# The last products of a two-layer backbone, taken a quarter of the tokens at a time for all four column tiles

## The chip, the cores and the metric

The program runs on one core of a Trainium2 chip. The metric is device time in microseconds (us) of one execution, over several executions of the same program; the trace is of one execution taken with the hardware profiler. The engines are named as the profile names them: PE is TensorE (matrix products), DVE is VectorE, ACT is ScalarE, POOL is GpSimd, SP is SyncE, whose queue issues the transfers.

## What is computed

Two layers over 1024 tokens of 1024 features, then a final RMS norm. Only the end of it matters here: the output projection of the second layer, the gated residual and the norm.

```python
def rmsnorm(x, g):
    xf = x.astype(jnp.float32)
    y = xf * lax.rsqrt(jnp.mean(xf * xf, axis=-1, keepdims=True) + RMS_EPS)
    return (y * g.astype(jnp.float32)).astype(x.dtype)
...
    return (y * jax.nn.silu(g)) @ p["w_out"]
...
        x = x + gate[:, None] * out_x
...
    return rmsnorm(x, final_g)
```

The norm of a token needs its squares over all 1024 features, so no output of a token can be written before its last feature is done.

## The kernel before

Features lie on the partitions, in eight column tiles of 128 (x[0] to x[7], 128 x 1024 tokens each); tokens lie along the free axis. HALF[0] is tokens 0 to 511, HALF[1] tokens 512 to 1023; `first` is 512 to 767 and `second` 768 to 1023, each a quarter of all tokens.

**Products.** A matrix product is made of 2 x 2 blocks by a scheme with seven block products. One pair of column tiles (m and m+1) and both halves of the tokens come out of the seven. Each block product (`prod`, L897 to L904) is 12 matmuls: four pieces of the inner dimension, and for each high x high, high x low and low x high parts of the operands. `last_half0` (L1546) makes five of the seven for one pair and so finishes HALF[0] of that pair. What is left for HALF[1] of a pair are two products: t1 (weights w[4]), whose result, copied out of the accumulator, completes tile m+1, and b22 (weights w[2]), accumulated on top of it, which completes tile m. The last two pairs are tiles 4, 5 (weights wa) and 6, 7 (weights wb).

**After a product.** `p5` (L1591) issues t1, has ACT copy the accumulator into a tile s3 (L1594), has DVE add gate times s3 to x (`gated`, L1422) and ACT square it (L1498). `p3` (L1598) issues b22 onto the same accumulator, which must therefore wait until the copy s3 has been read out, and then the same gated add, from PSUM, and a square. `fin_add` (L1504) adds a square to the sum `fin` of its half, on DVE.

**Norm.** `fin_cols` (L1507) sums `fin` over the partitions with small PE matmuls against ones (L1512, 128 tokens each) and takes the square root on ACT (`rc`, L1515). `fin_root` (L1518) takes the reciprocal and spreads it into a diagonal (`dg`), both on DVE (through `ordered`, L1494), broadcasts it over the partitions with a PE matmul (L1525) and copies that broadcast to SBUF on ACT (`rr`, L1527). `fin_out` (L1531) multiplies: tiles 1, 2, 3 on POOL with the copy rr (L1539), tiles 0, 4, 5, 6, 7 on DVE with the broadcast in PSUM (L1494), and stores groups of tiles with eight transfers on SP's queue (L1544), 512 KB each. DVE's first scaling of a root comes after ACT's copy of that root in the program's waits.

**What sets the order.** Each engine works its instructions in one fixed order. A scheduler lays that order out before the run; two chains in the code tie its hands. `product` (L1586) chains the block products in the order in which they are written, and `ordered` (L1490) chains DVE's adds, sums, reciprocals and scalings likewise. Before the change the written order is: t1 of tiles 4, 5 for the whole half (512 columns), t1 of tiles 6, 7 for each quarter, b22 of tiles 4, 5 for the whole half, b22 of tiles 6, 7 for each quarter. The root of HALF[0] and its scalings are written between these; the roots of the two quarters come after all of them.

Of the kernel before, what the change touches and what calls it, by code (L numbers as in the profile page):

```python
# [21 lines left out]
H = 512  # L22
HALF = (slice(0, H), slice(H, S))
# [32 lines left out]
def body(ctx, tc, xT, ctxT, cc, ccol, modT, modW, win, gw, wout, wu, grp, wg, wo1, small, edge, ident, outT):  # L56
# [18 lines left out]
    def dtile(name, dt=F32):  # L75
        return dpool.tile([P, S], dt, tag="d", name=name)
# [4 lines left out]
    def ttile(name):  # L81
        return tpool.tile([P, H], F32, tag="t", name=name)
# [4 lines left out]
    def psum(name):  # L87
        return pm.tile([P, H], F32, tag="mm", name=name)
# [27 lines left out]
    def wload(src, name, eng, n=D, out=None):  # L116
        raw = wpool.tile([P, n], F32, tag="wr", name=f"wr_{name}")
        load(raw, src)
        if out is None:
            hi = wpool.tile([P, n], F32R, tag="wh", name=f"wh_{name}")  # L120
            lo = wpool.tile([P, n], F32R, tag="wl", name=f"wl_{name}")
        else:
            hi, lo = out(f"wh_{name}", F32R), out(f"wl_{name}", F32R)
        split(raw, hi, lo, eng)
        return hi, lo
# [22 lines left out]
    def col(o, n=1):  # L148
        return sm[:, o : o + n]
# [326 lines left out]
    def raw_split(raw, name):  # L476
        hi = wpool.tile([P, D], F32R, tag="wh", name=f"wh_{name}")
        lo = wpool.tile([P, D], F32R, tag="wl", name=f"wl_{name}")
        cast(hi, raw)
        gp(out=lo, in0=raw, in1=hi.bitcast(F32), op=sub)  # L480
        return hi, lo
# [113 lines left out]
    with ExitStack() as actx:  # L595
# [77 lines left out]
        w = wload(win[3 * KT], "xb0", nc.gpsimd)  # L673
# [5 lines left out]
        w = wload(win[KT], "vg0", nc.gpsimd)  # L679
# [4 lines left out]
        for j in range(KT):  # L684
# [27 lines left out]
            if state is None:  # L712
                for m in range(2 * KT, 3 * KT):
                    part = L[m % 6][:, :D]
# [45 lines left out]
            for n, _ in enumerate(gate_steps(j, (gwh, gwl), (uh, ul), gates)):  # L760
# [3 lines left out]
                if n == 9:  # L764
                    w = raw_split(raw, name)
# [146 lines left out]
    def quad(w, name, ops, put, ahead=None):  # L912
        p1, p2, p3, p4, p5, p6, p7 = w
        a, c, b = psum(f"qa_{name}"), psum(f"qc_{name}"), psum(f"qb_{name}")
        prod(a, p1, ops["b11"], True, False)
        with tc.high_priority(offset=EVAC):
            evac = nc.scalar.copy(b, a)
        prod(c, p5, ops["t1"], True, False)
        with tc.high_priority(offset=EVAC):
            put(1, 1, c, 0)  # L920
        prod(b, p6, ops["t2"], False, False)
        with tc.high_priority(offset=EVAC):
            put(0, 1, b, 0)
        prod(a, p2, ops["b21"], False, True)
        with tc.high_priority(offset=EVAC):
            put(0, 0, a, None)
        w = None
        if ahead is not None:
            with tc.issue_after(evac.ins):
                w = ahead()  # L930
        prod(b, p7, ops["t3"], False, False)
        with tc.high_priority(offset=EVAC):
            put(1, 1, b, 1)
        prod(c, p3, ops["b22"], False, True)
        with tc.high_priority(offset=EVAC):
            put(0, 1, c, 1)
        prod(b, p4, ops["t4"], False, True)
        with tc.high_priority(offset=EVAC):
            put(1, 0, b, None)
        return w  # L940
# [90 lines left out]
    for m in range(KT):  # L1031
        w = gws[KT + m]
# [84 lines left out]
    for i in range(KH):  # L1117
        for j in (i, KH + i) if i else ():
            w = wload(win[2 * KT + j], f"ga{j}", nc.gpsimd)
# [224 lines left out]
    def wo1_weights(part, m):  # L1344
        return wquad([wo1[m + i, part] for i in range(2)], f"wo{part}_{m}", wo1_ring,
                     part == 1 and m >= KT - 4)
# [3 lines left out]
    for m in range(0, NK, 2):  # L1350
# [38 lines left out]
        elif m <= KT:  # L1389
            n = 2 * KT + m - 2  # L1390
# [9 lines left out]
        w = quad(wq, f"g{m}", bx, to_gate, (lambda: wo1_weights(0, 0)) if m == NK - 2 else None)  # L1400
# [24 lines left out]
    for m in range(0, KT, 2):  # L1425
# [28 lines left out]
        w = quad(w, f"wo0_{m}", yops[0], put, nxt)  # L1454
# [10 lines left out]
    for m in range(0, KT - 4, 2):  # L1465
# [12 lines left out]
        w = quad(w, f"wo1_{m}", yops[1], put, ahead)  # L1478
# [11 lines left out]
    def ordered(f, *args, **kw):  # L1490
        with ExitStack() as octx:
            if after[0] is not None:
                octx.enter_context(tc.issue_after(after[0].ins))
            after[0] = f(*args, **kw)  # L1494

    def square(k, cols):
        q = ttile(f"fq{k}_{cols.start}")[:, : cols.stop - cols.start]
        nc.scalar.activation(q, x1[k][:, cols], AF.Square)  # L1498
        return q
# [7 lines left out]
    def fin_cols(cols, ps):  # L1507
        n, h = cols.stop - cols.start, cols.start // H
        off, nt = cols.start - h * H, n // P
        sums = ps[0][:, :nt]  # L1510
        for c in range(nt):
            nc.tensor.matmul(sums[:, c : c + 1], fin[h][:, off + c * P : off + (c + 1) * P], ones[:, 0:1],  # L1512
                             start=True, stop=True)
        r = hpool.tile([P, nt], F32, tag=f"rc_{cols.start}", name=f"rc_{cols.start}")
        nc.scalar.activation(r, sums, AF.Sqrt, bias=eps_r)  # L1515
        return ps[1][:, -n:], r

    def fin_root(cols, root, r):  # L1518
        n = root.shape[-1]
        ordered(nc.vector.reciprocal, r, r)  # L1520
        t = ttile(f"dg_{cols.start}")[:, :n]
        ordered(nc.vector.tensor_tensor, out=t.rearrange("p (c t) -> p c t", t=P),
                in0=idD.unsqueeze(1).to_broadcast([P, n // P, P]),
                in1=r.unsqueeze(2).to_broadcast([P, n // P, P]), op=mult)
        nc.tensor.matmul(root, ones, t, start=True, stop=True)  # L1525
        rr = dtile(f"rr_{cols.start}")[:, :n]
        nc.scalar.copy(rr, root)  # L1527
        return root, rr


    def fin_out(cols, root, rr):  # L1531
        n = cols.stop - cols.start
        per = D // n
        for k0 in range(0, KT, per):
            o = dtile(f"o{cols.start}_{k0}").rearrange("p (k n) -> p k n", n=n)
            for k in range(k0, k0 + per):
                v = x1[k][:, cols]
                if k in GAINED:
                    nc.gpsimd.tensor_tensor(out=o[:, k - k0], in0=v, in1=rr, op=mult)  # L1539
                else:  # L1540
                    ordered(nc.vector.scalar_tensor_tensor, out=o[:, k - k0], in0=v, scalar=col(O_FG + k), in1=root,
                            op0=mult, op1=mult)
                    yield
            nc.sync.dma_start(outT[k0 : k0 + per, :, cols].rearrange("k p n -> p k n"), o)  # L1544
# [31 lines left out]
    m = KT - 4  # L1576
    wa = w
    wb, _, _ = last_half0(m, wa, ahead)
# [4 lines left out]
    first, second = slice(H, H + H // 2), slice(H + H // 2, S)  # L1583
    whole, local = slice(0, H), [slice(0, H // 2), slice(H // 2, H)]

    def product(w, op, c, part, start):  # L1586
        nonlocal mm
        with tc.issue_after(mm.ins):
            mm = prod_cols(c, w, ops[op], start, not start, part)

    def p5(m, w, c, part, cols):  # L1591
        product(w[4], "t1", c, part, True)
        s3 = ttile(f"s3_l{m}_{cols.start}")[:, : cols.stop - cols.start]
        nc.scalar.copy(s3, c[:, part])  # L1594
        ordered(gated, m + 1, x1[m + 1][:, cols], s3)
        return square(m + 1, cols)

    def p3(m, w, c, part, cols):  # L1598
        product(w[2], "b22", c, part, False)
        ordered(gated, m, x1[m][:, cols], c[:, part])  # L1600
        return square(m, cols)

    c4, c6 = psum("qc_l"), [psum(f"qc_l{n}") for n in range(2)]
    q5 = p5(m, wa, c4, whole, HALF[1])
    sums0 = fin_cols(HALF[0], fps[0])
    q7 = [p5(m + 2, wb, c6[0], local[0], first)]
    ordered(fin_add, HALF[1], q5)
    q7.append(p5(m + 2, wb, c6[1], local[1], second))
    root0 = fin_root(HALF[0], *sums0)
    q4 = p3(m, wa, c4, whole, HALF[1])  # L1610
    ordered(fin_add, first, q7[0])
    ordered(fin_add, second, q7[1])
    ordered(fin_add, HALF[1], q4)
    out0 = fin_out(HALF[0], *root0)
    q6 = [p3(m + 2, wb, c6[0], local[0], first)]
    next(out0)
    ordered(fin_add, first, q6[0])
    sums1 = fin_cols(first, fps[1])
    next(out0)
    q6.append(p3(m + 2, wb, c6[1], local[1], second))  # L1620
    next(out0)
    ordered(fin_add, second, q6[1])
    sums2 = fin_cols(second, [psum("fin_ms2")] * 2)
    root1 = fin_root(first, *sums1)
    for _ in out0:
        pass
    root2 = fin_root(second, *sums2)
    for cols, root in ((first, root1), (second, root2)):
        for _ in fin_out(cols, *root):
            pass  # L1630


def layout(i):
# [85 lines left out]
```

## Time and profile before

| | us |
|---|---|
| median of 3 runs | 1341.01 (1340.15 to 1341.77) |
| the profiled execution | 1340.89 |
| its span, first to last instruction | 1339.1 |
| mean granted TensorE clock | 0.985 |
| part of the span after the last block product's last matmul began (1321.81) | 17.3 |

The profile's page gives the busy time of each engine; the timeline gives single instructions with their start and length in us from the span's start, and in brackets the idle time of the engine just before and what ended it. A matmul's length includes a drain of 0.16 us that the next matmul does not wait for: the start-to-start distance is its cost on PE. A stage table gives, for each stretch of time, its length, each engine's busy time and count of instructions, the granted clock (PEclk), the share of the transfer engines and GB/s.

### The profile page before, as it was taken

What the parts mean: (1) busy time and instruction counts of PE and PEld (TensorE: products, weight loads), DVE (VectorE), ACT (ScalarE), POOL (GpSimd) and SP (SyncE); (2) the same over time, 40 slices, a digit from 0 to 9 for tenths busy, and PEclk for the clock granted to TensorE, in tenths of its full rate; (3) what the DMA queues carried; (4) which work ended last, traced back from release to release, by engine and by line L of the source; (5) the groups of instructions that cost most, each with busy time, mean ns of one, the idle gap of its engine ahead of it and who ended that gap; (6) DMA issues with size and microseconds to landing.
All of it is one profiled execution on the core that took longest, in us unless ns stands there. A gap on an engine that the chain in (4) does not pass through costs nothing.

```text
span 1339.1 us, 15886 instructions
## 1 busy us (share of the span) xinstructions
PE 1275.7 (95%) x5664; PEld 1039.6 (78%) x5664; DVE 1155.6 (86%) x1775; ACT 639.7 (48%) x924; POOL 344.1 (26%) x180
## 2 busy tenths in 40 slices
PE   7799999999999999969998999999999999999896
PEld 4478888888888887857887888788888888777684
DVE  7996999998999989999778767999999977877775
ACT  6353655666656623216534345744333434634442
POOL 5274443554436546532220023000000000000002
PEclk9999999999999999989998999999999999999997
DMA  9844111121111233432454446244333335767623
GB/s 359 295 142 165 41 47 56 56 71 40 63 56 56 79 126 115 161 126 79 155 173 141 170 172 197 87 149 150 107 115 118 116 113 163 262 213 250 220 102 126
DMA packets 82867, 181.80 MB, mean 136 GB/s; under 512 B 7778, under 2 KB 27618, under 8 KB 82788
## 3 DMA queue, kind: packets, MB, share of 16 engines
q1 hardware_dynamic: 74340, 176.60, 38.3%
q10 hardware_dynamic: 8448, 4.20, 1.1%
q8 instruction: 44, 0.72, 0.2%
q14 instruction: 35, 0.29, 0.1%
HBM read 136.72 MB, written 44.04 MB: 135 GB/s over the span
## 4 chain that ended last, share of the span: by engine, by line
PE 69%; DVE 15%; DMA 7%; ACT 3%; issue 2%; POOL 2%; SPq 0%; POOLq 0%; DVEq 0%; ACTq 0%
PE gb L445 7%; PE vg L445 6%; PE va L445 6%; PE xb L445 6%; DVE conv L445 4%; PE g L445 4%; PE wob L445 2%; PE ga L445 2%; PE ga L135 2%; PE ga L134 2%; PE ga L133 2%; DMA yr_t<-y_t 2%; DVE junk L219 2%; PE qb_g L901 1%; PE qb_g L904 1%
## 5 line engine op out<-in xcount | busy, mean ns | idle before, releaser
L445 DVE SCALAR_TENSOR_TENSOR conv<-u,sm,conv 128x505 f32<-128x505 f32 (+6 forms) x224 | 153.0, 745 | 0.8
L1539 POOL TENSOR_TENSOR o<-x,rr 128x256 f32<-128x256 f32 (+1 forms) x9 | 8.1, 933 | 457.7 <-ACT rr L1527 454.8
L445 ACT ACTIVATE l<-g,sm 128x512 f32<-128x512 f32 (+1 forms) x96 | 58.7, 619 | 58.8 <-PE g L445 58.1
L103 POOL TENSOR_TENSOR wl_wu<-wr_wu,wh_wu 128x1024 fp32r<-128x1024 f32 x16 | 38.9, 2434 | 153.9 <-ACT wh_wu L102 147.9
L256 PE MATMUL fold<-gh,wh_wu 128*128 128x512 f32 x128 | 53.4, 418 | 5.3 <-ACT wh_wu L102 5.3
L257 PE MATMUL fold<-gl,wh_wu 128*128 128x512 f32 x128 | 52.8, 413 | 3.7 <-DVE gl L103 3.7
L258 PE MATMUL fold<-gh,wl_wu 128*128 128x512 f32 x128 | 51.6, 412 | 2.5 <-POOL wl_wu L103 2.5
L445 POOL TENSOR_TENSOR l<-l,l 128x1280 f32<-128x1280 f32 x16 | 47.0, 2963 | 26.1 <-DVE conv L445 17.6
L445 PE MATMUL wob<-ybl,wh_wob 128*128 128x512 f32 x128 | 50.5, 394 | 3.0 <-POOL ybl L445 3.0
L102 ACT CAST wq_wo<-wr_wo 128x512 fp32r<-128x512 f32 x48 | 28.9, 619 | 48.4 <-DMA wr_wo<-wo 18.4
L445 PE MATMUL wob<-ybh,wh_wob 128*128 128x512 f32 x128 | 51.5, 403 | 0.0
L445 PE MATMUL wob<-ybh,wl_wob 128*128 128x512 f32 x128 | 50.1, 391 | 0.0
L445 PE MATMUL gb<-h0l,wh_gb 128*128 128x512 f32 x128 | 49.8, 389 | 0.0
L445 PE MATMUL gb<-h0h,wh_gb 128*128 128x512 f32 x128 | 49.8, 389 | 0.0
L445 PE MATMUL vg<-h0l,wh_vg 128*128 128x512 f32 x128 | 49.8, 389 | 0.0
L445 PE MATMUL vg<-h0h,wh_vg 128*128 128x512 f32 x128 | 49.8, 389 | 0.0
L445 PE MATMUL vg<-h0h,wl_vg 128*128 128x512 f32 x128 | 49.8, 389 | 0.0
L445 PE MATMUL va<-h0h,wh_va 128*128 128x512 f32 x128 | 49.8, 389 | 0.0
L445 PE MATMUL va<-h0l,wh_va 128*128 128x512 f32 x128 | 49.8, 389 | 0.0
L445 PE MATMUL va<-h0h,wl_va 128*128 128x512 f32 x128 | 49.8, 389 | 0.0
L445 PE MATMUL gb<-h0h,wl_gb 128*128 128x512 f32 x128 | 49.8, 389 | 0.0
L445 DVE TENSOR_TENSOR_SCAN l<-l,l 128x256 f32<-128x256 f32 (+1 forms) x32 | 48.7, 1521 | 1.1
(584 smaller groups left out, 4348.1 us busy)
## 6 DMA issues: line engine op xcount, KB each, us to landing
mod<-modT SPq DMA_DIRECT2D x20, 512.0 KB, 6.6
wr_wu<-wu SPq DMA_DIRECT2D x16, 512.0 KB, 4.1
x_part<-xp SPq DMA_DIRECT2D x32, 256.0 KB, 2.4
mod<-modT SPq DMA_DIRECT2D x32, 256.0 KB, 3.2
wr_v<-wfold SPq DMA_DIRECT2D x16, 512.0 KB, 3.6
wr_g<-wg SPq DMA_DIRECT2D x16, 512.0 KB, 4.9
wr_wo<-wo SPq DMA_DIRECT2D x16, 512.0 KB, 4.9
yr_t<-y_t SPq DMA_DIRECT2D x16, 512.0 KB, 6.5
```

The lines of the kernel that those rows point to most:

```text
L102: return (nc.scalar.copy(hi, src), eng.tensor_tensor(out=lo, in0=src, in1=hi.bitcast(F32), op=sub))
L103: eng.tensor_tensor(out=lo, in0=src, in1=hi.bitcast(F32), op=sub))
L133: nc.tensor.matmul(ps, hi[:, kc], xh[k][:, cols], start=(k == 0), stop=False)
L134: nc.tensor.matmul(ps, hi[:, kc], xl[k][:, cols], start=False, stop=False)
L135: nc.tensor.matmul(ps, lo[:, kc], xh[k][:, cols], start=False, stop=(k == ks - 1))
L219: nc.vector.scalar_tensor_tensor(out=junk, in0=raw, scalar=1.0, in1=vec, op0=mult, op1=mult, accum_out=t[:, i, m : m + 1])
L256: nc.tensor.matmul(ps, wh[:, kc], gh[i], start=(i == 0), stop=False)
L257: nc.tensor.matmul(ps, wh[:, kc], gl[i], start=False, stop=False)
L258: nc.tensor.matmul(ps, wl[:, kc], gh[i], start=False, stop=(i == 3))
L445: last[eng] = f(*args, **kw)
L901: nc.tensor.matmul(ps, hi, xh[k], start=(first and k == 0), stop=False, skip_group_check=not first)
L904: mm = nc.tensor.matmul(ps, lo, xh[k], start=False, stop=(k == KH - 1), skip_group_check=not first)
```

## The change

All four column tiles' products are made for one quarter of the tokens at a time: for `first` t1 of tiles 4, 5, t1 of tiles 6, 7, b22 of 4, 5, b22 of 6, 7, and then the same for `second`. So all products have 256 columns (96 matmuls of 256, where there were 24 of 512 and 48 of 256). A generator `half0`, advanced between the products of the first quarter, issues the sums, the root and the scalings of HALF[0]; `quarter0`, advanced between the products of the second quarter, issues what is left of them and then the root and scalings of the first quarter.

```diff
-    c4, c6 = psum("qc_l"), [psum(f"qc_l{n}") for n in range(2)]
-    q5 = p5(m, wa, c4, whole, HALF[1])
+
+    def quarter(cols, part, between):
+        n = cols.start // (H // 2)
+        cs = [psum(f"qc_l{q}_{n}") for q in range(2)]
+        qs = []
+        for q, w in enumerate((wa, wb)):
+            qs.append(p5(m + 2 * q, w, cs[q], part, cols))
+            next(between, None)
+        for q, w in enumerate((wa, wb)):
+            ordered(fin_add, cols, qs[q])
+            qs.append(p3(m + 2 * q, w, cs[q], part, cols))
+            next(between, None)
+        for q in (2, 3):
+            ordered(fin_add, cols, qs[q])
+
+    def half0():
+        yield
+        root0 = fin_root(HALF[0], *sums0)
+        yield
+        for _ in fin_out(HALF[0], *root0):
+            yield
+
     sums0 = fin_cols(HALF[0], fps[0])
-    q7 = [p5(m + 2, wb, c6[0], local[0], first)]
-    ordered(fin_add, HALF[1], q5)
-    q7.append(p5(m + 2, wb, c6[1], local[1], second))
-    root0 = fin_root(HALF[0], *sums0)
-    q4 = p3(m, wa, c4, whole, HALF[1])
-    ordered(fin_add, first, q7[0])
-    ordered(fin_add, second, q7[1])
-    ordered(fin_add, HALF[1], q4)
-    out0 = fin_out(HALF[0], *root0)
-    q6 = [p3(m + 2, wb, c6[0], local[0], first)]
-    next(out0)
-    ordered(fin_add, first, q6[0])
+    rest = half0()
+    quarter(first, local[0], rest)
     sums1 = fin_cols(first, fps[1])
-    next(out0)
-    q6.append(p3(m + 2, wb, c6[1], local[1], second))
-    next(out0)
-    ordered(fin_add, second, q6[1])
+
+    def quarter0():
+        next(rest, None)
+        root1 = fin_root(first, *sums1)
+        yield
+        for _ in rest:
+            yield
+        for _ in fin_out(first, *root1):
+            yield
+
+    rest1 = quarter0()
+    quarter(second, local[1], rest1)
     sums2 = fin_cols(second, [psum("fin_ms2")] * 2)
-    root1 = fin_root(first, *sums1)
-    for _ in out0:
+    for _ in range(3):
+        next(rest1, None)
+    root2 = fin_root(second, *sums2)
+    for _ in rest1:
         pass
-    root2 = fin_root(second, *sums2)
-    for cols, root in ((first, root1), (second, root2)):
-        for _ in fin_out(cols, *root):
-            pass
+    for _ in fin_out(second, *root2):
+        pass
```

What this does to the engines' orders shows at three places. In the rows below, the accumulators are named qc_l<pair>_<quarter> after the change (pair 0 is tiles 4, 5; quarter 2 is `first`, 3 is `second`); fq<tile>_<first token> is a square, s3_l<4 or 6>_<first token> a copied accumulator, fin_ms0, fin_ms1, fin_ms2 the roots of HALF[0], `first` and `second`, rr their copies, and o the scaled output.

ACT around the copy of the first root (rr_0). Before the change:

```order
L1498 ACTIVATE fq7_768_10450<-x2_7_10264 128x256
L1498 ACTIVATE fq4_512_10471<-x2_4_10148 128x512
L1527 COPY rr_0_10456<-fin_ms0_1_10389 128x512
L1498 ACTIVATE fq6_512_10489<-x2_6_10262 128x256
L1515 ACTIVATE rc_512_10496<-fin_ms1_10390,eps_r_121 128x2
L1498 ACTIVATE fq6_768_10519<-x2_6_10262 128x256
```

And ACT after the change:

```order
L1498 ACTIVATE fq4_512_10453<-x2_4_10148 128x256
L1527 COPY rr_0_10437<-fin_ms0_1_10389 128x512
L1498 ACTIVATE fq6_512_10471<-x2_6_10262 128x256
L1594 COPY s3_l4_768_10501<-qc_l0_3_10487 128x256
L1498 ACTIVATE fq5_768_10504<-x2_5_10150 128x256
L1515 ACTIVATE rc_512_10485<-fin_ms1_10390,eps_r_121 128x2
L1594 COPY s3_l6_768_10525<-qc_l1_3_10488 128x256
L1498 ACTIVATE fq7_768_10528<-x2_7_10264 128x256
```

Before, every s3 copy came ahead of rr_0. Now both s3 copies of the second quarter come behind it, the first behind the square of tile 6 as well, the second behind the square root of the first quarter's sums.

DVE at the same place, from the diagonal of the first root on, after the change:

```order
L1494 TENSOR_TENSOR dg_0_10434<-cH_3773,rc_0_10395 128x512
L1504 TENSOR_TENSOR fin1_10023<-fin1_10023,fq5_512_10414 128x256
L1422 SCALAR_TENSOR_TENSOR x2_4_10148<-qc_l0_2_10397,m1_162,x2_4_10148 128x256
L1494 SCALAR_TENSOR_TENSOR o0_0_10455<-x2_0_9879,sm_115,fin_ms0_1_10389 128x512
L1504 TENSOR_TENSOR fin1_10023<-fin1_10023,fq7_512_10431 128x256
L1422 SCALAR_TENSOR_TENSOR x2_6_10262<-qc_l1_2_10398,m1_162,x2_6_10262 128x256
L1494 SCALAR_TENSOR_TENSOR o0_4_10479<-x2_4_10148,sm_115,fin_ms0_1_10389 128x512
L1504 TENSOR_TENSOR fin1_10023<-fin1_10023,fq4_512_10453 128x256
L1504 TENSOR_TENSOR fin1_10023<-fin1_10023,fq6_512_10471 128x256
```

DVE before the change had, around its first scaling:

```order
L1504 TENSOR_TENSOR fin1_10023<-fin1_10023,fq4_512_10471 128x512
L1422 SCALAR_TENSOR_TENSOR x2_6_10262<-qc_l0_10392,m1_162,x2_6_10262 128x256
L1494 SCALAR_TENSOR_TENSOR o0_0_10491<-x2_0_9879,sm_115,fin_ms0_1_10389 128x512
L1504 TENSOR_TENSOR fin1_10023<-fin1_10023,fq6_512_10489 128x256
L1494 SCALAR_TENSOR_TENSOR o0_4_10504<-x2_4_10148,sm_115,fin_ms0_1_10389 128x512
```

The first scaling (o0_0) stood behind the gated add of tile 6 of the first quarter; now it stands ahead of it.

PE after the change, where the first root's broadcast stands among the second quarter's t1 products of tiles 6, 7, and the first b22 product behind it:

```order
L901 MATMUL qc_l1_3_10488<-y1_t1h1_9711,wq_wo1_6_5_10256 128x256
L1525 MATMUL fin_ms0_1_10389<-dg_0_10434,ones_119 128x512
L903 MATMUL qc_l1_3_10488<-y1_t1l1_9712,wq_wo1_6_5_10256 128x256
L904 MATMUL qc_l1_3_10488<-y1_t1h1_9711,wq_wo1_6_5_10256 128x256
L901 MATMUL qc_l1_3_10488<-y1_t1h1_9711,wq_wo1_6_5_10256 128x256
L903 MATMUL qc_l1_3_10488<-y1_t1l1_9712,wq_wo1_6_5_10256 128x256
L904 MATMUL qc_l1_3_10488<-y1_t1h1_9711,wq_wo1_6_5_10256 128x256
L901 MATMUL qc_l0_3_10487<-y1_b22h0_9954,wq_wo1_4_3_10145 128x256
```

Seven of these twelve t1 matmuls come ahead of the broadcast. The sums of the first quarter (L1512) stand between the two b22 products of the second quarter, and its root's broadcast behind the last of them. Before the change the broadcast stood among the very last products, and both quarters' sums and broadcasts behind them all.

## The prediction

> **What bounds the kernel now.** First the page's busy times and its chain of waits, then a stage table of the end, which is all that the change touches.
>
> ```profile
> span 1339.1 us, 15886 instructions
> ...
> PE 1275.7 (95%) x5664; PEld 1039.6 (78%) x5664; DVE 1155.6 (86%) x1775; ACT 639.7 (48%) x924; POOL 344.1 (26%) x180
> ...
> PE 69%; DVE 15%; DMA 7%; ACT 3%; issue 2%; POOL 2%; SPq 0%; POOLq 0%; DVEq 0%; ACTq 0%
> ```
>
> ```profile
> 1308.98:1321.93 12.95, 12.95 (x83) 11.46 (x81) 7.84 (x15) 6.23 (x13) 0.09 (x1) 1.00 0.00 0
> 1321.93:1332.85 10.92, 4.04 (x14) 2.38 (x12) 10.42 (x22) 1.84 (x6) 7.96 (x9) 0.65 0.63 230
> 1332.85:1339.10 6.25, 0.00 (x0) 0.00 (x0) 0.00 (x0) 0.00 (x0) 0.01 (x1) 0.50 0.81 269
> ```
>
> PE is the bound of the whole. The columns of the second view are the stretch, its length, busy time of PE, PEld, DVE, ACT and POOL, the granted clock, the transfers' share and GB/s. While the last products run (1308.98 to 1321.93) PE is busy for all 12.95 us and DVE for 7.8; behind them DVE is busy for 10.4 of 10.9 us with sums, roots and scalings; then 6.25 us are transfers alone. So the change can win in the 17.2 us behind the products (to 1339.1), and lose where PE has no gap today. The landmarks there:
>
> ```profile
> 1321.81 0.28 PE L904 MATMUL qc_l<-y_b22h,wq_wo 128*128 128x256 f32 x1
> 1325.03 1.01 DVE L1504 TENSOR_TENSOR fin<-fin,fq 128x256 f32<-128x256 f32 x1
> 1329.79 0.37 ACT L1527 COPY rr<-fin_ms 128x256 f32<-128x256 f32 x1 [1.21 <-PE fin_ms L1525]
> 1333.10 1.11 SPq L1544 DMA_DIRECT2D outT<-o  x1
> ...
> DMA to landing us min/median/max: 5.1/5.1/5.1
> DMA to landing us min/median/max: 2.8/2.8/2.8
> ```
>
> The last add of squares ends at 1326.04, the last root's copy at 1330.16, 4.1 us on. The last store, issued at 1333.10, lands 5.1 us later (1338.2), for it queues behind others; the first, alone, took 2.8 (last row). From the last landing to the end of the span are 0.9 us.
>
> **The change, step by step.** Durations come from these groups of 1309 to 1339.1 (mean ns at the end):
>
> ```profile
> L1539 POOL TENSOR_TENSOR o<-x,rr 128x256 f32<-128x256 f32 x6 | 4.2, 736 | 3.0 <-issue 3.0
> L1494 DVE SCALAR_TENSOR_TENSOR o<-x,sm,fin_ms 128x256 f32<-128x256 f32 x10 | 4.0, 473 | 0.2 <-ACT rr L1527 0.2
> L1494 DVE SCALAR_TENSOR_TENSOR o<-x,sm,fin_ms 128x512 f32<-128x512 f32 x5 | 3.6, 739 | 0.8 <-ACT rr L1527 0.8
> L1504 DVE TENSOR_TENSOR fin<-fin,fq 128x256 f32<-128x256 f32 x4 | 2.7, 693 | 0.0
> ...
> L1498 ACT ACTIVATE fq<-x 128x256 f32<-128x256 f32 x4 | 1.7, 416 | 0.7 <-DVE x L1422 0.7
> L1422 DVE SCALAR_TENSOR_TENSOR x<-qc_l,m,x 128x256 f32<-128x256 f32 x2 | 1.0, 476 | 0.0
> L1594 ACT COPY s_l<-qc_l 128x256 f32<-128x256 f32 x2 | 0.7, 364 | 0.3 <-PE qc_l L904 0.3
> L1515 ACT ACTIVATE rc<-fin_ms,eps_r 128x2 f32<-128x2 f32 x2 | 0.5, 262 | 4.2 <-PE fin_ms L1512 4.2
> ```
>
> ```profile
> 1308.98 0.39 PE L901 MATMUL qc_l<-y_t1h,wq_wo 128*128 128x512 f32 x1
> 1311.70 0.28 PE L901 MATMUL qc_l<-y_t1h,wq_wo 128*128 128x256 f32 x1
> 1311.82 0.28 PE L903 MATMUL qc_l<-y_t1l,wq_wo 128*128 128x256 f32 x1
> ...
> 1313.86 0.95 PE L1512 MATMUL fin_ms<-ones,fin 128*128 128x1 f32 x8
> 1314.67 0.36 PE L901 MATMUL qc_l<-y_t1h,wq_wo 128*128 128x256 f32 x1
> ...
> 1320.12 1.02 PE L1525 MATMUL fin_ms<-dg,ones 128*128 128x512 f32 x2
> ...
> 1321.10 0.28 PE L904 MATMUL qc_l<-y_b22h,wq_wo 128*128 128x256 f32 x1
> ```
>
> *Splitting the 512-wide products.* 12 matmuls of 512 take 2.72 us (1308.98 to 1311.70), of 256 they take 12 x 0.12 = 1.44; 24 become 48, which adds 2 x (2.88 - 2.72) = 0.3 us of PE. The sums of HALF[0] cost PE 0.81 (1313.86 to 1314.67), its root's broadcast 0.86 (1320.12 to 1321.10, less one product of 0.12), as before. The sums of `first`, half as many, come in among the products: 0.4. So if PE never waited, the products would end at 1308.98 + 8 x 1.44 + 0.81 + 0.86 + 0.4 = 1322.6, where they end at 1321.93 now: **+0.7**.
>
> *The first wait.* The first quarter's four products and the sums end at 1308.98 + 4 x 1.44 + 0.81 = 1315.55; t1 of tiles 4, 5 follows to 1316.99, seven more matmuls to 1317.83, then the broadcast; its result is out at 1318.85, the other five t1 matmuls are issued by 1319.29. The next product, b22 onto the accumulator of tiles 4, 5, needs ACT's copy s3 of it. That copy has been possible since 1317.2 but stands third on ACT: behind rr, and behind the square of tile 6, for which DVE must first do its scaling o0, an add and the gated add. What these cost together, these rows show:
>
> ```profile
> 1321.18 0.59 ACT L1527 COPY rr<-fin_ms 128x512 f32<-128x512 f32 x1 [1.29 <-PE fin_ms L1525]
> 1321.80 0.75 DVE L1494 SCALAR_TENSOR_TENSOR o<-x,sm,fin_ms 128x512 f32<-128x512 f32 x1 [0.78 <-ACT rr L1527]
> 1322.46 0.93 DVE L1504 TENSOR_TENSOR fin<-fin,fq 128x256 f32<-128x256 f32 x1
> ...
> 1321.84 1.27 POOL L1539 TENSOR_TENSOR o<-x,rr 128x512 f32<-128x512 f32 x1 [454.76 <-ACT rr L1527]
> 1323.07 1.45 POOL L1539 TENSOR_TENSOR o<-x,rr 128x512 f32<-128x512 f32 x1
> 1324.49 1.26 POOL L1539 TENSOR_TENSOR o<-x,rr 128x512 f32<-128x512 f32 x1
> ```
>
> DVE's scaling starts only when rr is there. The add behind it (both inputs in SBUF) takes 0.93 us while POOL scales; it ends 0.28 behind the end of POOL's instruction (1323.11, 1323.39), and the one of 1.01 us above does the same (1325.75, 1326.04): **a DVE add waits for the POOL instruction under way**. Walked through: rr 1318.9 to 1319.5; o0 to 1320.2 beside POOL's first; the add ends at 1320.8 + 0.28 = 1321.05; gated add 0.48, to 1321.5; square 0.42, to 1321.9; s3 copy 0.36, ready at 1322.2. PE waits from 1319.3 to 1322.2: **+2.9**. Nothing can cover that, since PE's order has only this product next. Were the adds free of POOL, it would be 2.4.
>
> *The second wait.* b22 of tiles 4, 5, then the sums of `first` on PE, for which DVE's last add of `first` must be done. DVE does o4 to 1322.15; one add ends with POOL's second instruction, one with its third, at 1323.9. After the sums (0.4), the square root (0.26), and the next s3 copy (0.36) behind it on ACT, b22 of tiles 6, 7 may start: about 1.1 us after the sums begin. PE waits some 0.7 us there.
>
> *The clock.* What waits do to it, these rows show:
>
> ```profile
> 72.00:73.00 1.00, 0.54 (x1) 0.50 (x2) 1.00 (x2) 0.74 (x2) 1.00 (x2) 0.71 0.12 32
> 75.00:76.00 1.00, 1.00 (x4) 0.76 (x4) 1.00 (x2) 1.00 (x2) 1.00 (x1) 0.59 0.25 90
> 720.00:721.00 1.00, 0.60 (x2) 0.16 (x2) 1.00 (x3) 0.00 (x0) 0.00 (x0) 0.97 0.00 0
> 1325.00:1326.00 1.00, 0.00 (x0) 0.00 (x0) 1.00 (x3) 0.00 (x0) 0.75 (x1) 0.55 0.43 160
> ```
>
> ```profile
> 69.01:72.42 3.41, 1.52 (x6) 0.67 (x4) 3.41 (x5) 3.41 (x8) 2.58 (x2) 1.00 0.54 154
> 1195.39:1198.81 3.42, 1.64 (x7) 1.37 (x8) 3.42 (x6) 0.73 (x2) 0.00 (x0) 1.00 0.50 158
> ```
>
> The granted clock falls to half at 72.42 (0.71 as the mean of that us) and returns at 75.82, 3.40 later; it falls again at 720.94 and 1325.10, which are 190 and 177 steps of 3.413 us on. So it is decided once in 3.41 us, by the steps just ended: with PE busy for 1.52 us (45%) it fell, with 1.64 (48%) it did not. If the changed kernel meets the same steps, the one from 1318.27 to 1321.68 has PE busy for 1.2 us only (to 1319.45, drain included), 35%, and the clock is halved until 1325.10. With another phase it falls too unless a step begins between about 1320.6 and 1321.2 (mod 3.41), some 8 in 10. No 256-wide product at half clock stands in the trace; bounds are 0.12 (no effect) and 0.24 us (all of it), and I take the upper, since the clock's row says half. b22 of tiles 4, 5 then runs from 1322.2 to 1325.05 instead of 1323.65: **+1.4**. The sums follow, root and copy to 1326.2, the last product to 1327.65. That is 1321.93 + 0.7 + 2.9 + 1.4 + 0.7: **the products end 5.7 us later**.
>
> *Behind the products.* Root broadcast (0.5) and rr (0.37) of `first` are done at 1328.65, when POOL starts its three scalings of 0.74. DVE, busy since the square root at 1325.9 with seven instructions, still has an add, the gated add of tile 6, o512_0 and two adds to do, each add held by a POOL instruction: the last ends at about 1331.8. From there to the last root's copy took 4.1 us before; there DVE's scaling o7 stood ahead of the reciprocal, and two broadcasts in place of one, so I take 3.5, to 1335.3. Five DVE scalings (4.0 for ten) take 2.05: the store of these is issued at 1337.4, POOL's right behind. Now both are late, so that nothing queues ahead: 2.8 for the first, 1.6 more for the second (512 KB at 269 / 0.81 = 332 GB/s, the rate of the last stage while transfers ran), 0.9 to the end: **1342.7**. From the products' end to the span's are 15.05 us instead of 17.2, so 2.1 are won behind and 5.7 lost ahead. Sum: **+3.6**.
>
> The early stores of HALF[0] and `first` cost nothing: the transfers stand idle beside them. The generators cost nothing on the chip. Bounds: the clock 0 to 1.4, the holds of POOL 0 to about 1.7, phase of the clock at the last sums ±0.4.
>
> **Rivals.**
>
> *The clock stays up* (PE's waits as above). The Trainium skill, "TensorE: Matmul & The Clock Gate", Part 1: The HAM clock gate (the "warmup" mystery), has the half clock come after at least one idle window of about 3.4 us; by that, a wait of 2.9 us would not do it. The trace disagrees: a window with PE busy for 1.52 us dropped it. Worked out without the halving, all behind 1322.2 comes 1.1 us sooner: the span is 1341.6, +2.5, the run 1343.4. For it: the phase may differ.
>
> *POOL doesn't hold DVE's adds.* The first wait is 2.4, the second vanishes, the last adds come 1 us sooner: about +0.9, 1341.8. Against it: two adds of 0.93 and 1.01 us where the other two of the four take 0.41 (4 x 0.693, less these, halved).
>
> *The products run through* and the change gives what it is written for. Then they end at 1322.6; the last gated add, square and add take 1.3 us (0.8 more if held), 3.5 to the last root, 2.05, and 2.8 + 1.6 + 0.9: 1336, -3, 1337.9, **faster**. One thing decides: that the copy s3 of tiles 4, 5 in the second quarter is ready by 1319.3. In ACT's order it isn't, unless the first broadcast comes out 2.9 us sooner, which PE's order excludes; only if copy and square were done out of order.
>
> That the change does not do what it says is half true already: the root of `first` comes behind the last product, so only its sums lie beside them.
>
> **How the numbers follow.** The forecast is 1340.89 + 3.6 = 1344.5 (the profiled execution; the median of the runs is 1341.01). Chances: waits with half clock 0.54, with full clock 0.26, adds not held 0.11, products run through 0.09. About 0.2%, 2.7 us, is what a measurement of this kernel can tell from no change: above 1343.7 is slower, below 1338.3 faster. The first case lies above for nine parts of ten, the second, at 1343.4 with an error of 1, for three, the third within, the fourth below: slower 0.56, same 0.35, faster 0.09. The range reaches from the third case with the phase's 0.2 off, 1341.6, to the forecast plus the 1.2 us that phase and holds leave open, 1345.7.
>
> **What would show it.** PE idle for nearly 3 us just before the second quarter's first b22 matmul, ended by ACT's copy L1594; behind that product a granted clock of 0.5; DVE idle for 3 us before its first scaling, and adds of 0.7 us and more beside POOL; the last product's end near 1327.6; the last two stores issued within 0.5 us. Wrong would be a PE wait under 1 us there, or a clock that stays at 1.00, or adds of 0.41 us beside POOL.

## The result, and the profile after

| | before | changed | ratio (95% interval) |
|---|---|---|---|
| first comparison: median, us | 1341.77 (1340.15 to 1346.01, 7 runs) | 1351.08 (1345.53 to 1355.91, 7 runs) | 1.006 (1.004 to 1.008) |
| all comparisons pooled: median, us | 1343.9 (1338.86 to 1349.13, 122 runs) | 1347.95 (1343.64 to 1355.91, 53 runs) | by job, below |
| tail of the profiled executions, us | 30.12, 29.83, 29.84 | 34.09, 33.83, 34.05, 34.07, 33.86, 34.08 | |

The changed kernel is slower: 9.3 us by the medians of the first comparison, 4.1 us when the runs of all comparisons are pooled. A job is below one set of versions run together on one chip; the three jobs of the experiments ran on three different chips. "Tail" is here the time from the first matmul of the last products (tile qc_l, L901) to the end of the span. The forecast was 3.6 us slower, 1344.5; the measured 1351.08 lies outside its range.

The first profile of the changed kernel is of the execution of 1345.53 us, the fastest of the seven (span 1343.7). Its stages, with the columns of the stage table shown of before (stretch, length, busy PE, PEld, DVE, ACT, POOL, granted clock, share of the transfers, GB/s):

```profile
1309.61:1322.95 13.34, 10.53 (x83) 9.84 (x81) 7.33 (x14) 5.42 (x12) 2.70 (x3) 1.00 0.04 14
1322.95:1329.11 6.16, 5.54 (x29) 5.31 (x30) 5.67 (x12) 1.36 (x4) 1.40 (x1) 0.61 0.60 225
1329.11:1336.32 7.21, 3.19 (x9) 1.69 (x8) 4.75 (x11) 1.63 (x5) 2.46 (x3) 0.50 0.47 166
1336.32:1343.70 7.38, 0.00 (x0) 0.00 (x0) 2.05 (x5) 0.00 (x0) 2.09 (x3) 0.50 0.58 193
```

In before the last products began at 1308.98 and PE was busy for every one of their 12.95 us. Here they begin at 1309.61 and take 19.5 us; in the first of these stretches PE idles for 2.8 of 13.34 us, in the next the clock is at 0.61 on average. The rows behind that, from the timeline (start, length, engine, line, operation; in brackets the idle time before and what ended it):

```profile
1309.61 0.28 PE L901 MATMUL qc_l<-y_t1h,wq_wo 128*128 128x256 f32 x1
...
1319.58 0.59 ACT L1527 COPY rr<-fin_ms 128x512 f32<-128x512 f32 x1 [2.23 <-PE fin_ms L1525]
1320.20 0.75 DVE L1494 SCALAR_TENSOR_TENSOR o<-x,sm,fin_ms 128x512 f32<-128x512 f32 x1 [3.36 <-ACT rr L1527]
1320.87 0.93 DVE L1504 TENSOR_TENSOR fin<-fin,fq 128x256 f32<-128x256 f32 x1
1321.72 0.47 DVE L1422 SCALAR_TENSOR_TENSOR x<-qc_l,m,x 128x256 f32<-128x256 f32 x1
...
1322.23 0.42 ACT L1498 ACTIVATE fq<-x 128x256 f32<-128x256 f32 x1 [2.06 <-DVE x L1422]
1322.55 0.35 ACT L1594 COPY s_l<-qc_l 128x256 f32<-128x256 f32 x1
1322.95 0.39 PE L901 MATMUL qc_l<-y_b22h,wq_wo 128*128 128x256 f32 x1 [2.82 <-ACT s_l L1594]
1323.18 0.28 PE L903 MATMUL qc_l<-y_b22l,wq_wo 128*128 128x256 f32 x1
1323.30 0.28 PE L904 MATMUL qc_l<-y_b22h,wq_wo 128*128 128x256 f32 x1
...
1326.32 0.58 PE L901 MATMUL qc_l<-y_b22h,wq_wo 128*128 128x256 f32 x1 [0.61 <-ACT s_l L1594]
...
1328.83 0.41 PE L904 MATMUL qc_l<-y_b22h,wq_wo 128*128 128x256 f32 x1
1329.04 1.05 PE L1525 MATMUL fin_ms<-dg,ones 128*128 128x256 f32 x2
...
1335.91 0.37 ACT L1527 COPY rr<-fin_ms 128x256 f32<-128x256 f32 x1 [2.03 <-PE fin_ms L1525]
...
1338.39 0.92 SPq L1544 DMA_DIRECT2D outT<-o  x2
```

Read downwards, this is one chain: the copy rr, DVE's first scaling (idle 3.36 us for it), the held add of 0.93 us, the gated add of tile 6, its square, the copy s3, and then PE, which had waited 2.82 us. A second wait of 0.61 us follows. And the clock, in the table of PE alone (stretch, length, busy PE, granted clock, share of the transfers, GB/s):

```profile
1320.87:1324.28 3.41, 1.32 (x11) 1.00 0.41 154
1324.28:1327.69 3.41, 2.80 (x14) 0.50 0.71 267
1327.69:1331.10 3.41, 2.41 (x10) 0.50 0.43 162
```

A step of 3.41 us in which PE is busy for 1.32 (39%) ends at 1324.28 with the clock halved, when eleven of the twelve matmuls of the first b22 product are issued. So nearly all of that product runs at the full clock and the next one, from 1326.32, at half.

### The profile page after: what moved, and what is told of

It is laid out like the page before. It is cut to its first block, busy times and chain, and to the rows that moved or that the text cites. A ratio compares the mean times of both kernels' runs of the same rounds, so it can differ in the third digit from the quotient of the medians.

```text
span 1343.7 us, 15941 instructions
## 1 busy us (share of the span) xinstructions
PE 1279.4 (95%) x5688; PEld 1042.5 (78%) x5688; DVE 1158.7 (86%) x1779; ACT 639.7 (48%) x927; POOL 345.2 (26%) x180
## 4 chain that ended last, share of the span: by engine, by line
PE 63%; DVE 19%; DMA 9%; ACT 3%; issue 3%; POOL 2%; SPq 0%; POOLq 0%; DVEq 0%; ACTq 0%
PE gb L445 6%; PE vg L445 6%; PE va L445 6%; PE xb L445 6%; DVE conv L445 4%; PE g L445 4%; PE wob L445 2%; PE ga L445 2%; PE ga L134 2%; PE ga L133 2%; PE ga L135 2%; DMA yr_t<-y_t 1%; DVE ws L1273 1%; PE xbc L445 1%; DMA wr_g<-wg 1%
```

## The experiments

Two things were asked: whether the waits of PE, as the prediction has them, make the tail longer, and where the rest of 9.3 us comes from.

**again and null**: the changed kernel and before once more, unchanged, in one job with the two that follow.

> The changed kernel once more, nothing edited. Tail = from the first last-product matmul (qc_l) to the end of the span: 30.1 us before the change, 34.1 in the profile of the changed kernel (+4.0, the forecast was +3.6). Theory A (the change costs its tail, the other 5 us of the measured median are spread between executions that any version of this kernel has): tail 33 to 35 again, median 3 to 6 us above the kernel before in the same rounds. Theory B (the changed program also runs its earlier part, up to the first qc_l matmul at 1309 to 1310, slower in most executions): median 8 us or more above, with the kernel before staying in its own 1340 to 1346.

> The kernel before, against itself: ratio 1.000 by every theory. Its spread is what A needs: executions up to 1346 or higher, with the start of the last products moved by several us between two profiles of one program.

Measured: again 1350.38 us (6 runs), ratio 1.0044 (1.0028 to 1.006), tail 33.83: its median lies 6.2 us over before's, just beyond theory A's 3 to 6 and short of theory B's 8. Null 1343.93 us (12 runs), ratio 0.9999 (0.9986 to 1.0013), tail 29.83. Before's own median in this job is 1344.2 over 29 runs, from 1340.84 to 1348.06: the three runs known at first, 1340.15 to 1341.77, stand at the low edge of that. So some 2.4 us of the 9.3 were a low sample of before (1341.77 in the first comparison). The rest left a gap: 4.0 us of tail against 6 us of time.

**root**: the first root's broadcast goes onto PE ahead of all products of the second quarter; nothing moves on ACT and DVE.

```diff
-        nc.tensor.matmul(root, ones, t, start=True, stop=True)
+        bc = nc.tensor.matmul(root, ones, t, start=True, stop=True)
+        if cols == HALF[0]:
+            mm_root[0] = bc
...
     rest1 = quarter0()
+    mm = mm_root[0]
     quarter(second, local[1], rest1)
```

> One edit: the first root's broadcast on PE comes ahead of the second quarter's products instead of behind 19 of their matmuls; ACT and DVE keep their orders. Theory of the wait (rr and the scaling behind it hold the copy s3, so PE): rr 2.2 us sooner, PE's wait before the first b22 product of the second quarter 0.5 to 0.8 us instead of 2.8, no halved clock ahead of that product, tail 31 us, 3 us under the changed kernel and within 1.5 us of the kernel before. Rival (DVE and POOL work beside the products is the bound, not the wait): tail stays within 1 us of 34.1. Theory B adds that the time stays 5 us over its tail.

Measured: 1344.46 us (12 runs), ratio to before 1.0002 (0.9989 to 1.0015), tail 30.51. Its timeline of PE and its stages (products, then what lies behind them):

```profile
1324.91 0.39 PE L901 MATMUL qc_l<-y_b22h,wq_wo 128*128 128x256 f32 x1 [0.57 <-ACT s_l L1598]
...
1327.92 0.38 PE L901 MATMUL qc_l<-y_b22h,wq_wo 128*128 128x256 f32 x1 [0.65 <-ACT s_l L1598]
```

```profile
1313.79:1329.45 15.66, 14.38 (x111) 13.41 (x110) 11.77 (x22) 6.65 (x16) 4.14 (x3) 1.00 0.23 87
1329.45:1344.30 14.85, 2.40 (x10) 1.22 (x8) 8.00 (x19) 1.74 (x5) 4.66 (x6) 0.66 0.55 191
```

With one matmul earlier on PE the first wait falls from 2.82 to 0.57 us, the clock stays at 1.00 through the products, and 3.5 of the tail's 4.07 us are gone (30.51, where the changed kernel has 34.0 on average). The long wait and the halved clock behind it are thus most of what the change costs, and the place of the broadcast on PE decides whether they come. The edit does not make the quarters a gain: before with the same edit (broot, below) has a tail of 28.59.

**warm**: twelve matmuls of 512 columns, into an accumulator that is free there, fill PE's wait; everything else as changed.

```diff
+        if cols == second:
+            with tc.issue_after(mm.ins):
+                mm = prod(fps[0][0], wa[4], ops["t1"], True, True)
         for q, w in enumerate((wa, wb)):
             ordered(fin_add, cols, qs[q])
```

> The changed kernel with 12 idle matmuls of 512 columns (2.7 us of PE, their result is not used) where PE waits for 2.8 us, into the accumulator that held the first sums. Theory of the clock: the granted clock stays at 1.00 through both b22 products of the second quarter, these take 1.44 us each instead of 1.5 and 2.6, the tail is 32.6 to 33.3 us. Rival (what follows the products is bound elsewhere and the clock costs nothing): tail within 0.4 us of 34.1.

Measured: 1345.3 us (12 runs), ratio 1.002 (1.0007 to 1.0034), tail 33.12. Timeline and stage of the products:

```profile
1325.75 0.40 PE L901 MATMUL fin_ms<-y_t1h,wq_wo 128*128 128x512 f32 x1
...
1328.76 0.39 PE L901 MATMUL qc_l<-y_b22h,wq_wo 128*128 128x256 f32 x1
```

```profile
1315.38:1333.40 18.02, 17.20 (x124) 15.59 (x123) 11.87 (x22) 6.67 (x16) 4.16 (x3) 1.00 0.21 77
```

The first b22 product begins 13.38 us behind the first product, as in the changed kernel (13.34), but the clock stays up and the last product comes 1.4 us sooner (17.82 against 19.22 us behind the first). Of that the end of the span gets 0.9 us. Work that computes nothing shortens the tail here, because it keeps the clock; with the clock kept, the wait itself costs as much as before.

**nopool**: POOL's scalings of HALF[0] become a fill with zeros, which runs long before, so that no POOL instruction stands beside DVE's adds of the first quarter. The kernel leaves out the scaled tiles 1 to 3 of HALF[0]; POOL's scalings of the two quarters stay.

```diff
-                    nc.gpsimd.tensor_tensor(out=o[:, k - k0], in0=v, in1=rr, op=mult)
+                    if cols == HALF[0]:
+                        nc.gpsimd.memset(o[:, k - k0], 0.0)
+                    else:
+                        nc.gpsimd.tensor_tensor(out=o[:, k - k0], in0=v, in1=rr, op=mult)
```

> Leaves out part of the computation: POOL's scalings of tiles 1 to 3 of the first half (three 128x512 multiplications behind rr) are replaced by filling those parts of the output tile with zero, early. Orders of PE, ACT and DVE are those of the changed kernel. Theory A (POOL holds DVE's adds, and the adds hold the square of tile 6 and with it the s3 copy that PE waits for): the adds of the first quarter take 0.41 us instead of 0.9, PE's first wait falls from 2.8 to about 1.8 us; tail 32.6 (31.7 to 33.6) if the clock still falls, 31 if it doesn't. The rival on record priced this at 2.7 us less than the changed kernel (tail about 31). Theory C (the order on ACT and DVE alone makes the wait, POOL's hold is hidden behind rr): adds shorter, but first wait still 2.6 to 2.8 and tail 33.5 to 34.

Measured: 1347.59 us (12 runs), ratio 1.0024 (1.0011 to 1.0038), tail 33.44. Timeline of DVE, ACT and PE:

```profile
1323.12 0.42 DVE L1504 TENSOR_TENSOR fin<-fin,fq 128x256 f32<-128x256 f32 x1
...
1321.83 0.59 ACT L1527 COPY rr<-fin_ms 128x512 f32<-128x512 f32 x1 [2.23 <-PE fin_ms L1525]
1323.96 0.42 ACT L1498 ACTIVATE fq<-x 128x256 f32<-128x256 f32 x1 [1.54 <-DVE x L1422]
1324.29 0.35 ACT L1597 COPY s_l<-qc_l 128x256 f32<-128x256 f32 x1
...
1324.69 0.39 PE L901 MATMUL qc_l<-y_b22h,wq_wo 128*128 128x256 f32 x1 [2.31 <-ACT s_l L1597]
```

The add takes 0.42 us instead of 0.93, so POOL does hold it. But from rr's start to the copy's start there are still 2.46 us where there were 2.97; the wait shrinks by 0.51 us and the tail by 0.6, where this run's expectation had 1 and 1.4, and the rival on record 2.7 us of time. The hold is real and small. Neither theory's numbers fit: the wait lies between A's 1.8 and C's 2.6 to 2.8; it is the 2.4 that the prediction gives for adds free of POOL. The other 2.3 us come from the order. Moving the copy s3 alone ahead on ACT was not tried.

**broot**: the edit of root, made in before (the broadcast ahead of the products of b22 of tiles 6, 7).

> Before with one edit: the first root's broadcast (the 128x512 matmul into fin_ms0) is put on PE ahead of the products of b22 for tiles 6 and 7; in before it stands inside the second of them. ACT and DVE orders are those of before. Theory A (the tail is set by how soon rr and the scalings of the first half get onto DVE, ACT and POOL): rr comes some 2 us earlier, tail 28.8 instead of 29.9, time 1 us less (ratio 0.999). Rival: the scalings of the first half are hidden in before anyway, and PE's products end 0 to 1 us later for waiting for the diagonal: tail 30 to 31, ratio 1.000 to 1.001.

Measured: 1343.98 us (12 runs), the median of before in that job, ratio 0.9994 (0.9978 to 1.0009), tail 28.59: 1.3 us shorter than before's 29.93 on average, as theory A had it, though rr comes only 1.4 us sooner (10.81 against 12.20 us behind the first product) where it had 2; the last product still starts 12.83 us behind the first. The time can't show a gain of that size: the interval holds both 1 us less and no change.

**again2**, in the same job as nopool, broot and best: the changed kernel a third time.

> The changed kernel once more, to settle how much of its loss lies in the last products and the tail. Tail here means the time from the first matmul of the last products (tile qc_l, L901) to the end of the span: 30.1 and 29.8 us in the two profiles of before so far, 34.1 and 33.8 in the two of the changed kernel. Theory A (the whole loss is made in the tail, as the record's steps have it): tail 33.5 to 34.3, median 4 us over that of before in the same job (ratio 1.003), and the 6 us of the first two jobs were a matter of sampling. Theory B (something ahead of the tail is slower too): median 6 us or more over before (ratio 1.0045 or more) with a tail that is still 34.

Measured: 1347.68 us (12 runs) against 1343.98 (35 runs), ratio 1.0023 (1.001 to 1.0035), tail 34.05. So here the time, 3.7 us, agrees with the tail, 4.1.

**look1, look2, look3, lookb**: three more profiles of the changed kernel and one of before, to see whether the tail varies as the times do.

> The changed kernel unchanged, one of three more profiles of it. What is open: its tail (first matmul of the last products to the end of the span) was 34.1, 33.8 and 34.05 us in three profiles, 4 us over before, but its times stood 3.7, 6 and 9 us over before in three jobs. Theory A (the loss of the tail is the same in every execution, and the rest of the scatter is made ahead of it, in code that the change doesn't touch): tail 33.5 to 34.3, whatever the time. Theory E (in some executions the clock falls earlier in the tail and costs more): a tail of 35 or more in one of the three, in the execution with the lower mean clock (0.978 or less).

> As look1, with the same kernel: A tail 33.5 to 34.3; E 35 or more in one of the three.

> As look1 and look2: A tail 33.5 to 34.3; E 35 or more in one of the three. Over the three, median 3.3 to 4.5 us over before of the same job by A.

> Before unchanged, a third profile of it: A tail 29.7 to 30.3 wherever the tail begins; a ratio of 1 within 0.002.

| | median us (runs) | ratio (95%) | mean clock of the profiled execution | its first product begins | its tail |
|---|---|---|---|---|---|
| look1 | 1347.51 (10) | 1.0023 (1.0011 to 1.0036) | 0.977 | 1311.33 | 34.07 |
| look2 | 1346.84 (10) | 1.0031 (1.0012 to 1.005) | 0.982 | 1310.74 | 33.86 |
| look3 | 1348.88 (8) | 1.0048 (1.0029 to 1.0066) | 0.974 | 1314.62 | 34.08 |
| lookb | 1343.91 (10) | 1.0011 (0.9993 to 1.0028) | 0.982 | 1311.96 | 29.84 |

Theory A holds, E falls: the execution with a clock of 0.974 has the same tail as the others, and its lateness is there already when its first product begins. The six tails of the changed kernel lie within 0.26 us, the three of before within 0.29; their means are 34.0 and 29.93, **4.07 us** apart. The medians of all runs are 4.1 us apart. Medians for the same changed kernel differ by up to 3.5 us between sets of runs (1346.84 to 1350.38, and 1351.08 in the first comparison), by 2.0 within one job. No execution above 1350.5 us was profiled, so what the longest ones (to 1355.91) did isn't shown, and what makes the executions differ ahead of the products was not tried.

**best**: the quarters of the change, with the order written out on PE, ACT and DVE (helpers named by what they issue: T and B the products t1 and b22 of pair and quarter, C the copy s3, X5, X3 the gated adds, Q, A squares and their adds, MS, RC, RT, RR the sums, root, broadcast and copy, O scalings). Squares, copies and diagonals lie in buffers of their own.

```diff
+    tX5(0, 0), tQ(1, 0), tA(1, 0)
+    tT(1, 0), tMS(0), tRC(0), tC(1, 0), tDG(0)
+    tB(0, 0), tRT(0), tX5(1, 0), tQ(3, 0), tX3(0, 0), tQ(0, 0), tA(3, 0), tA(0, 0)
+    tRR(0), tO(0, 1, 2, 3), tB(1, 0), tO(0, 4), tO(0, 5), tX3(1, 0), tQ(2, 0), tO(0, 0), tA(2, 0)
+    tST(0, 0), tST(0, 2), tST(0, 4)
+    tT(0, 1), tC(0, 1), tT(1, 1), tO(0, 7), tMS(1), tRC(1), tX5(0, 1), tO(0, 6), tST(0, 6)
...
+    tB(0, 1), tA(1, 1), tX3(0, 1), tQ(0, 1), tB(1, 1), tA(3, 1), tX3(1, 1), tRT(1), tRR(1), tO(1, 1, 2, 3)
```

> The quarters of the changed kernel with the order of the last instructions written out on PE, ACT and DVE: the first root's broadcast between the products of b22 for tiles 4,5 and 6,7 of the first quarter; the sums of the first quarter between t1 and b22 of the second; each s3 copy of the second quarter ahead of the square root and the squares that wait for DVE's adds; the squares, s3 copies and diagonals in buffers that are free by then, so that none waits for the four buffers of tile t. The computation is whole. Theory A (quarter by quarter loses only by PE's two waits and the clock step they cost, so that with the waits gone the shorter work behind the last product is left as a gain): PE waits under 0.5 us in the last products, clock 1.00 through the last b22 product, last product ends 13 us behind the first, tail 25.5 to 26.5, time 3.5 to 4.5 us less than before (ratio 0.997) and 7.5 to 8.5 less than the changed kernel. Theory D (DVE's and the stores' work behind the last product is what ends the kernel, whatever PE does): tail 29 to 30, ratio 0.999 to 1.000.

Measured: 1341.46 us (12 runs) against 1343.98, ratio 0.998 (0.9966 to 0.9995), tail 25.87. Stages and timeline (PE, ACT):

```profile
1314.93:1328.83 13.90, 13.90 (x112) 13.42 (x111) 12.27 (x25) 7.17 (x17) 3.99 (x3) 1.00 0.34 126
1328.83:1334.00 5.17, 1.71 (x8) 0.85 (x7) 4.29 (x11) 1.41 (x5) 2.44 (x4) 1.00 0.37 131
1334.00:1340.80 6.80, 0.00 (x0) 0.00 (x0) 1.83 (x5) 0.00 (x0) 1.92 (x3) 0.53 0.78 260
```

```profile
1320.13 1.08 PE L1591 MATMUL fin_ms<-dg,ones 128*128 128x512 f32 x2
...
1324.11 0.37 ACT L1591 COPY s<-qc_l 128x256 f32<-128x256 f32 x1
...
1325.71 0.36 PE L901 MATMUL qc_l<-y_b22h,wq_wo 128*128 128x256 f32 x1
...
1328.55 0.28 PE L904 MATMUL qc_l<-y_b22h,wq_wo 128*128 128x256 f32 x1
```

PE is busy for all 13.90 us; the copy is done 1.2 us before the product that needs it. The tail is 4.1 us shorter than before's and 8.1 shorter than the changed kernel's. The time gains 2.5 us in this job, less than the tail and than the 3.5 to 4.5 expected, within an interval that holds both; this version beats both kernels. Orders on three engines and buffers change at once here, so what each of them brings isn't shown.

## Why the prediction was wrong, point by point

**The step that failed is its last sum**, "The forecast is 1340.89 + 3.6 = 1344.5 (the profiled execution; the median of the runs is 1341.01)". The measured 1351.08 is 6.6 us above it: 3.0 lie in the base, 0.5 in the 3.6, and 3.1 in the first comparison itself, whose cause stays open. Term by term:

- *The base, 1340.89.* Before's median is 1343.9 over 122 runs that go from 1338.86 to 1349.13. The first products begin anywhere from 1308.98 to 1315.51 us in the fourteen profiles, whose code up to that point no edit touches (nopool's fill with zeros apart). The one of the prediction was the earliest of all. From 1343.9, the same sum gives 1347.5; the changed kernel's median over all runs is 1347.95.
- *The range, 1341.6 to 1345.7.* It took in the unknown terms of the tail and nothing of this scatter. The first comparison's 1351.08, seven runs from 1345.53 to 1355.91, stands another 3.1 us above the median of all 53; its two longest executions have the lowest mean clocks of the seven, 0.974 and 0.977. What lowered them there isn't shown.
- *The sum, +3.6.* Measured +4.07, by tails. The path it describes is the one in the trace, and of its signs only the last product's end is off (1329.0 for 1327.6); the term that it has too small is the waits' cost on PE.

Within the sum:

- *The waits, +2.9 and +0.7.* PE's idle time is 2.82 us, ended by the copy s3 as named (2.8 in all six profiles of the changed kernel), and 0.61. But the waits cost PE about 4.1 us and not 3.6: the last product starts 19.22 us behind the first, before 12.83, so 6.39 later, of which the clock is 1.5 and the splitting 0.8 (both below). The bracketed idle times add up to 3.43; two things make most of the other 0.7. The idle time is counted only from the end of the drain of 0.16 us, and the first matmul behind a wait takes 0.23 us to the next at full clock (1322.95 to 1323.18) where the others take 0.12.
- *Splitting, +0.7*: in best, where PE never waits, the products take 0.8 us more than before's (13.62 against 12.83 from the first one's start to the last one's). Right.
- *The clock, +1.4*: from the start of the second quarter's first b22 product to that of the last matmul there are 5.88 us here, and 4.42 in root and 4.44 in warm, where the clock stays at 1.00. So the clock costs 1.5: the size is right, but partly by luck. The forecast had the clock fall before that product, slow it to half, and return behind it. In the first profile the clock fell as that product was nearly over, did not return one step of 3.41 us later, and halved the next product instead (2.72 us from 1326.32 to 1329.04). In again and look2 it went as forecast, and there the same stretch is 5.49 and 5.45 (1.0 us for the clock); in look1, where the clock falls halfway through the first of the two products, it is 6.13 (1.7).
- *Behind the products, -2.1*: 14.87 us from the last product's start to the end, before 17.29 in the profile predicted from, so -2.4 (17.00 in the two other profiles of before, so -2.1 by them).
- *The rivals.* "The clock stays up" was priced at 1.1 us less than the forecast; warm, which keeps it up, has 0.9 us less of tail. "POOL doesn't hold DVE's adds" fell as a mechanism. Of its price of 2.7 us nopool tests the part of the first quarter's adds: the first wait is 2.31, near the 2.4 it had, and the tail gives 0.6. The second wait does not vanish: in nopool the last of the first quarter's adds ends at 1325.44, a microsecond before PE reaches the sums (1326.49), and PE still idles for 0.61 us, for the sums, the square root and the copy s3, which the forecast's own 0.7 is made of too. The last adds, which still stand beside POOL's scalings of `first`, are not freed in nopool. "The products run through" was refused for this order, rightly; with an order in which they do, in best, the tail is 4.1 us shorter than before's, where the rival had 3.

On pages: the Trainium skill, "TensorE: Matmul & The Clock Gate", HAM oscillation — how this bites in real kernels, gives as the abstract rule that PE should have no idle gaps over about 3.4 us. This trace disagrees: the clock was halved with no gap longer than 2.82 us, behind a step of 3.41 us in which PE was still busy for 39%. The Trainium skill, "SBUF — State Buffer", Who interferes with whom, says that a DVE instruction with two SBUF inputs contends with a GpSimd instruction that reads SBUF and not with one that only writes it; 0.93 us beside POOL's multiplication and 0.42 without it agree with the first part; no run here shows the second, for nopool's fill was over long before the adds.

## What to carry to other kernels

Work that is moved in beside another stage brings its waits with it: before pulling a root, a scaling or a copy forward, read on each engine what will stand ahead of the one instruction that the bound engine needs next, and write that order out if the scheduler doesn't. A change at the end of a long kernel is measured by its own stage over a few profiles (4.07 us, within 0.3) rather than by whole times that scatter by 10 us, and a forecast of the time has to start from the median of many runs, with their scatter in its range.

## What the runs showed of the hardware

In the last products the clock fell behind steps that were less than half busy: 39% in the first profile (above), 24% in again, 23 to 46% over the six profiles of the changed kernel. It came back only behind fuller ones. From again, in the table of PE alone, the step before the fall, the halved step, and the moment of its return:

```profile
1320.87:1324.28 3.41, 0.83 (x6) 1.00 0.08 29
1324.28:1327.70 3.42, 3.18 (x15) 0.50 0.58 221
```

```profile
1327.40:1327.60 0.20, 0.20 (x4) 0.50 1.00 379
1327.60:1327.80 0.20, 0.20 (x3) 0.77 1.11 420
```

A halved step with PE busy for 3.18 us (93%) brought the clock back, and so did 3.12 us in look2 and 3.21 in look1; 2.80 us (82%) in the first profile did not, nor 2.75 to 2.81 in look1, look3, again2 and nopool. So with the same wait the clock's phase decides whether it returns after one slow step; of the tail this is worth only 0.2 us (33.83 and 33.86 against 34.05 to 34.09), though the products end 0.4 us sooner. What takes up the other 0.2 isn't shown.

No share of busy time marks the border for the whole kernel, neither the 45 and 48% that the prediction reads from before nor the ones here. In null the clock fell behind a step with PE busy for 1.84 us (1261.55 to 1264.96, 54%) and stayed up behind one with 1.55 (1155.73 to 1159.14, 45%). In before a halved step with 2.87 us (62.18 to 65.59, 84%) brought it back, and in look3 one that was busy throughout by the profile (39.32 to 42.73, 3.41 us) did not. What the clock counts beyond that isn't shown.
